# Feed-forward pairs: two of seven weight remainders on GpSimd, and a 4 KB scratch for dynamic DMAs

## Chip, cores and metric

One core of a Trainium2 chip runs the whole kernel. The metric is the device time of one execution in microseconds. The engines are named as in the profile: PE is TensorE (PEld its weight loads), DVE VectorE, ACT ScalarE, POOL GpSimd, SP the engine that issues most of the DMAs.

## What is computed

A two-layer encoder on 512 tokens of width 1024, in fp32. Each layer is a feed-forward, a mixer (attention of two kinds), attention to a memory, and a second feed-forward. The change touches the four feed-forwards alone:

```python
def swiglu(x, wg, wu, wd):
    return (jax.nn.silu(x @ wg) * (x @ wu)) @ wd

for layer in range(DEPTH):
    h = h + 0.5 * swiglu(rmsnorm(h, g), wg, wu, wd)      # ffn1
    h = h + mixer(rmsnorm(h, mix_g), ...)
    h = h + memory_xattn(rmsnorm(h, mg), rmsnorm(mem, sg), ...)
    h = h + 0.5 * swiglu(rmsnorm(h, g), wg, wu, wd)      # ffn2
```

wg and wu are 1024 x 2816, wd is 2816 x 1024.

## The kernel before

**Numbers in two parts.** A matrix product in fp32 is done as three products of numbers in a shorter form (fp32r in the code). Each operand t is split into h, its rounding to that form, and l = t - h, the remainder; the product is h·h + h·l + l·h. For a weight tile, ScalarE makes h (an activation that copies, L519 in the pairs, L167 elsewhere) and VectorE makes l (a tensor_sub, L520 and L169). In the mixers some of the L169 subtractions are given to GpSimd (`wshare`). In the feed-forwards `wshare` is 0, so there all are on VectorE.

**Pairs.** The 22 blocks of 128 hidden columns of wg and wu are taken two at a time. Pair 0 is plain (`plain_pair`). The other ten pairs of a feed-forward, p = 1 to 10, use a seven-product scheme (Strassen's) on 2 x 2 quarters: the weights of a pair come as four quarters of 128x1024, and the tokens as four quarters and four prepared sums. The products of a pair, in the order in which TensorE runs them, with the tokens' name in quotes:

- `open_pair`: "11" with quarter 0 (w11), into bank y
- `sum_pair`: "1" with quarter 2 + quarter 3 (s), into bank z; "2" with s - w11 (L580), into y
- `cross_pair`: "21" with **quarter 1** (w12), into a bank of its own; "3" with quarter 0 - quarter 2, into y
- then `open_pair` of the next pair
- `close_pair`: `lower`, "4" with **quarter 3**, into y; `upper`, "22" with w12 - s (L623), into z. In the last pair `upper` comes first.

Between the products into y and z the bank is copied into `gu` by ScalarE (L564, L587, L608, L619) or added to it by VectorE (L597, L609, L627). The pair ends with the gates (L656, Silu at L658, L659) and the split of the hidden values (L429 on ScalarE, L433 on VectorE).

A product (`product`, L541) is 24 matmuls of 128x128 weights on 256 columns: two halves of the output, in each four blocks with h·h, four with the tokens' l, four with the weights' l. So the weights' l is first read by the ninth matmul. The operand of a product lies in one of three places: two buffers of the tiles `wh`/`wl`, and one pair of own tiles `sh`/`sl` for every third.

**Sums made by DMA.** Quarter 2 + quarter 3 and quarter 0 - quarter 2 are made by a plain fetch on SP's queue (L528) followed by an accumulating DMA that GpSimd issues (L574, L603); for the second, ScalarE negates the fetched quarter first (L602). [...]

**First pair.** The prepared token sums are made at the start of a feed-forward (`token_sums`, L452) and split at first use (L459 on ScalarE, L462 and L464 on VectorE). R, the row of normalising factors, is copied from PSUM by VectorE (L406). In this pair the operand of "21" is queued by hand behind the remainder of "2":

```python
with self.tc.high_priority(), self.behind(f.lowered if p == 1 else None):
    pair.w12 = self.raw_quarter(p, 1)
    w = self.operand(pair.w12)
```

`behind(ins)` is `issue_after`: what the block issues on the engine of `ins` comes behind `ins` on that engine; it adds no wait, and nothing on other engines is held.

**Order of work.** TensorE's order is the order of the program. On the other engines a scheduler sets the order beforehand, from a simulated timeline, and takes work under `high_priority` first. On the chip every engine runs its queue in order, with waits on semaphores.

After pairs 4 and 8 and in the last, `down` multiplies the hidden values with wd (L685), with the results scaled by R and added to x (L695, L696).

Of the kernel before, what the change touches and what calls it, by code (L numbers as in the profile page):

```python
# [11 lines left out]
F32 = mybir.dt.float32  # L12
# [99 lines left out]
class Encoder:  # L112
# [392 lines left out]
        f.own = True  # L505
        return tiles

    def operand(self, t, own=None):

        nc, f = self.nc, self.f  # L510
        if own is None:
            own = f.n % 3 == 2
            f.n += 1
        if own:
            h, l = self.own_tiles()
        else:
            h, l = [self.wp.tile([P, 1024 + WHOLE], F32R, name=n, tag=n, bufs=2)[:, o:o + 1024]
                    for n, o in (("wh", LINE), ("wl", LINE + STEP))]
        self.leading = nc.scalar.activation(h, t, AF.Copy)  # L519
        self.parted = nc.vector.tensor_sub(l, t, h.bitcast(F32))  # L520
        return h, l

    def quarter(self, p, q):
# [65 lines left out]
    def cross_pair(self, pair):  # L589
        nc, f, p = self.nc, self.f, pair.p  # L590
        with self.tc.high_priority(), self.behind(f.lowered if p == 1 else None):
            pair.w12 = self.raw_quarter(p, 1)
            w = self.operand(pair.w12)
        x = self.bank("pa")
        self.product(x, w, self.tokens("21"), True)
        c = self.corner(pair, 0, 0)
        nc.vector.tensor_add(c, c, self.halves(x))  # L597
        with self.tc.high_priority():
            s = f.tp.tile([P, 1024], F32, name="s3", tag="s3", bufs=2)
            self.fetch(s, p, 2)  # L600
            with self.behind(f.led), self.behind(f.taken):
                nc.scalar.activation(s, s, AF.Copy, scale=-1.0)  # L602
            nc.gpsimd.dma_start(s, self.quarter(p, 0), accum_op=OP.add)  # L603
            w = self.operand(s)
            f.crossed = self.parted
        self.product(pair.y, w, self.tokens("3"), False)
        c = self.corner(pair, 1, 1)
        f.taken = nc.scalar.copy(c, self.halves(pair.y))  # L608
        nc.vector.tensor_add(c, c, self.halves(pair.z))  # L609

    def close_pair(self, pair, final):
        nc, f, p = self.nc, self.f, pair.p
        own = False if final else None

        def lower():
            with self.tc.high_priority():
                w = self.operand(self.raw_quarter(p, 3), own)
            self.product(pair.y, w, self.tokens("4"), False)
            nc.scalar.copy(self.corner(pair, 1, 0), self.halves(pair.y))  # L619

        def upper():
            with self.tc.high_priority(), self.behind(f.crossed if p == 1 else None):
                nc.vector.tensor_sub(pair.s, pair.w12, pair.s)  # L623
                w = self.operand(pair.s, own)
            self.product(pair.z, w, self.tokens("22"), False)
            c = self.corner(pair, 0, 1)
            nc.vector.tensor_add(c, c, self.halves(pair.z))  # L627

        gu = pair.gu.rearrange("p (b z t) -> p b z t", b=2, z=2)
        if final:  # L630
            gs2 = f.tp.tile([P, 1024], F32, name="gs", tag="gs")
            t2 = f.tp.tile([P, 1024], F32, name="t", tag="t")

            def gate(b):
                gs, t = (x[:, b * S:(b + 1) * S] for x in (gs2, t2))
                nc.vector.tensor_mul(gs, gu[:, b, 0, :], f.R)
                nc.scalar.activation(t, gs, AF.Silu)
                nc.vector.tensor_mul(gs, t, gu[:, b, 1, :])
                return gs

            upper()
            with self.tc.high_priority():
                gs = gate(0)
            lower()
            with self.tc.high_priority():
                self.hidden_parts(p, gs, 0)
                self.hidden_parts(p, gate(1), 1)
            return
        lower()
        upper()  # L650

        def gates(after=None):
            gs = f.tp.tile([P, 1024], F32, name="gs", tag="gs")
            two = lambda t: t.rearrange("p (b t) -> p b t", b=2)
            with self.behind(after):
                nc.vector.tensor_mul(two(gs), gu[:, :, 0, :], f.R.unsqueeze(1).to_broadcast([P, 2, S]))  # L656
            t = f.tp.tile([P, 1024], F32, name="t", tag="t")
            nc.scalar.activation(t, gs, AF.Silu)  # L658
            nc.vector.tensor_mul(two(gs), two(t), gu[:, :, 1, :])  # L659
            self.hidden_parts(p, gs, 0)  # L660

        return gates
# [1077 lines left out]
```

## Time and profile before

| | |
|---|---|
| time, median of 3 runs | 2048.16 us (2047.85 to 2049.57) |
| profiled execution, its own time | 2049.99 us |
| its span | 2048.2 us |
| granted TensorE clock | 0.999 |
| busy: PE, DVE, ACT, POOL | 2039.4, 1516.7, 1142.3, 356.5 us |
| share of the chain that ended last: PE | 96% |
| L520 on DVE, in all | 280 instructions of 1.22 us |
| L169 on POOL (mixers) | 43 instructions |
| accumulating DMAs that POOL issues | 80 |

Rows of the profile read as: start, duration, engine, line, operation, output <- inputs, shapes, count, and in brackets the idle time before it with what ended it. A group's row has minimum/median/maximum in ns. A row of waits has who waited, for whom, us in total, times, and the longest.

### The profile page before, as it was taken

The numbers are of one execution on the slowest core, as the hardware profiler recorded it, in microseconds if no ns is written. First come the engines' busy times: TensorE is split into PE (matmuls) and PEld (weight loads), VectorE is DVE, ScalarE is ACT, GpSimd is POOL, SyncE is SP. The second block draws the span as 40 slices with busy tenths as digits, with TensorE's granted clock in tenths as the row PEclk, the third lists the DMA queues.
The fourth block names the chain that finished last, engine by engine and source line by source line (L and its number), as shares of the span: only waits on it lengthen the run. The fifth ranks groups of instructions, "written<-read, shape, count | busy, mean of one in ns | idle before, by whom it ended". The sixth has DMA issues, their size and how long they took to land.

```text
span 2048.2 us, 32531 instructions
## 1 busy us (share of the span) xinstructions
PE 2039.4 (100%) x12845; PEld 1825.0 (89%) x12845; DVE 1516.7 (74%) x2199; ACT 1142.3 (56%) x1719; POOL 356.5 (17%) x323
## 2 busy tenths in 40 slices
PE   9999999999999999999999999999999999999999
PEld 7989898888888899998989899988888888989997
DVE  8858577799676797685789576685668688958676
ACT  7636354556785664462556264454768566626443
POOL 1101003355521110010020000013353111001000
PEclk9999999999999999999999999999999999999999
DMA  7847545322332176483456476444224324747543
GB/s 222 224 117 193 144 116 167 98 88 83 104 122 69 52 216 165 135 204 105 118 170 183 127 180 168 124 124 147 93 83 127 100 73 144 190 120 189 161 121 95
DMA packets 87272, 279.64 MB, mean 137 GB/s; under 512 B 9808, under 2 KB 13008, under 8 KB 87120
## 3 DMA queue, kind: packets, MB, share of 16 engines
q1 hardware_dynamic: 75312, 235.09, 35.5%
q0 software_dynamic: 11520, 41.95, 11.8%
q8 instruction: 101, 1.65, 0.3%
q14 instruction: 51, 0.42, 0.1%
q10 hardware_dynamic: 288, 0.52, 0.1%
HBM read 271.24 MB, written 6.29 MB: 135 GB/s over the span
## 4 chain that ended last, share of the span: by engine, by line
PE 96%; DVE 1%; DMA 1%; ACT 1%; issue 0%; POOL 0%; SPq 0%; DVEq 0%; POOLq 0%; ACTq 0%
PE ps_pa L541 26%; PE ps_pa L797 13%; PE ps_pa L685 12%; PE ps_pb L685 12%; PE ps_pb L541 11%; PE ps_pa L743 5%; PE ps_pb L910 3%; PE ps_pa L386 2%; PE ps_pa L1398 2%; PE ps_pa L1231 2%; PE ps_pb L963 1%; PE ps_pb L743 1%; PE ps_pb L936 1%; PE ps_pa L1130 1%; PE ps_pb L386 1%; DMA wf<-l_ffn_wq 1%
## 5 line engine op out<-in xcount | busy, mean ns | idle before, releaser
L167 ACT ACTIVATE wh<-wf 128x1024 fp32r<-128x1024 f32 (+2 forms) x219 | 216.2, 992 | 350.8 <-PE ps_pb L685 92.3
L169 DVE TENSOR_TENSOR wl<-wf,wh 128x1024 fp32r<-128x1024 f32 (+2 forms) x176 | 203.8, 1161 | 42.4 <-ACT wh L167 38.6
L519 ACT ACTIVATE wh<-s 128x1024 fp32r<-128x1024 f32 x108 | 114.9, 1064 | 110.3 <-PE ps_pa L541 41.0
L520 DVE TENSOR_TENSOR wl<-s,wh 128x1024 fp32r<-128x1024 f32 x108 | 132.1, 1223 | 58.7 <-ACT wh L519 57.1
L603 POOL DMA_DIRECT2D s<-l_ffn_wq x40 | 34.8, 870 | 761.6 <-ACT s L602 717.5
L519 ACT ACTIVATE wh<-wf 128x1024 fp32r<-128x1024 f32 x84 | 88.9, 1058 | 91.6 <-PE ps_pa L685 30.2
L797 PE MATMUL ps_pa<-wh,xh 128*128 128x512 f32 x384 | 121.7, 398 | 0.0
L797 PE MATMUL ps_pa<-wh,xl 128*128 128x512 f32 x384 | 118.9, 391 | 0.0
L797 PE MATMUL ps_pa<-wl,xh 128*128 128x512 f32 x384 | 118.7, 390 | 0.0
L169 POOL TENSOR_TENSOR wl<-wf,wh 128x1024 fp32r<-128x1024 f32 (+1 forms) x43 | 95.6, 2224 | 128.9 <-ACT wh L167 128.6
L695 DVE TENSOR_TENSOR dn<-ps_pa,R 128x512 f32<-128x512 f32 x48 | 33.1, 689 | 97.5 <-PE ps_pa L685 97.2
L520 DVE TENSOR_TENSOR wl<-wf,wh 128x1024 fp32r<-128x1024 f32 x84 | 102.5, 1221 | 3.1 <-ACT wh L519 3.1
L685 PE MATMUL ps_pb<-hh,wh 128*128 128x512 f32 x352 | 96.2, 389 | 0.0
L685 PE MATMUL ps_pb<-hl,wh 128*128 128x512 f32 x352 | 96.1, 389 | 0.0
L685 PE MATMUL ps_pb<-hh,wl 128*128 128x512 f32 x352 | 96.0, 389 | 0.0
L520 DVE TENSOR_TENSOR sl<-s,sh 128x1024 fp32r<-128x1024 f32 x52 | 64.4, 1239 | 33.3 <-ACT sh L519 33.1
L685 PE MATMUL ps_pa<-hh,wh 128*128 128x512 f32 x328 | 88.9, 390 | 0.0
L685 PE MATMUL ps_pa<-hl,wh 128*128 128x512 f32 x328 | 88.6, 389 | 0.0
L685 PE MATMUL ps_pa<-hh,wl 128*128 128x512 f32 x328 | 88.6, 389 | 0.0
L254 POOL TENSOR_TENSOR acc<-acc,sq 128x512 f32<-128x512 f32 (+1 forms) x31 | 46.6, 1504 | 237.0 <-ACT sq L253 236.4
L797 PEld LDWEIGHTS ps_pa<-wh,xl 128*128 128x128 f32 x384 | 72.1, 188 | 15.7
L797 PEld LDWEIGHTS ps_pa<-wl,xh 128*128 128x128 f32 x384 | 72.0, 188 | 15.6
(403 smaller groups left out, 5774.9 us busy)
## 6 DMA issues: line engine op xcount, KB each, us to landing
wf<-l_ffn_wq SPq DMA_DIRECT2D x120, 512.0 KB, 3.9
s<-l_ffn_wq SPq DMA_DIRECT2D x80, 512.0 KB, 4.6
s<-l_ffn_wq POOLq DMA_DIRECT2D x80, 512.0 KB, 7.4
wf<-l_ffn_wd SPq DMA_DIRECT2D x64, 512.0 KB, 4.4
wf<-l_w_in SPq DMA_DIRECT2D x48, 512.0 KB, 3.3
wf<-l_ffn_wd SPq DMA_DIRECT2D x32, 384.0 KB, 3.1
wf<-l_w_out SPq DMA_DIRECT2D x16, 512.0 KB, 3.3
bias<-bias SPq DMA_DIRECT2D x28, 256.0 KB, 2.7
```

What stands on the lines that cost most here:

```text
L167: self.leading = nc.scalar.activation(wh[:, sl], w[:, sl], AF.Copy)
L169: eng.tensor_sub(wl[:, sl], w[:, sl], wh.bitcast(F32)[:, sl])
L254: self.summed = (eng or nc.gpsimd).tensor_add(acc[:, :n], acc[:, :n], sq[:, :n])
L386: nc.tensor.matmul(p, w[a][:, k * P:(k + 1) * P], xs[k][c], start=k == order[0] and a == c == 0, stop=k == order[-1] and a == 1)
L519: self.leading = nc.scalar.activation(h, t, AF.Copy)
L520: self.parted = nc.vector.tensor_sub(l, t, h.bitcast(F32))
L541: self.nc.tensor.matmul(bank[:, sl], w[a][:, o:o + P], xs[k][b], start=first and z == a == b == k == 0, stop=z == a == 1 and k == KB // 2 - 1,
L685: self.nc.tensor.matmul(bank, w[a][:, j * P:(j + 1) * P], h, start=j == a == e == 0, stop=j == nb - 1 and (a, e) == ops[-1])
L743: nc.tensor.matmul(banks[dd], w[g, k // 2][a][:, o:o + P], parts(k)[b], start=k == first and a == b == 0, stop=k == last and a == 1)
L797: nc.tensor.matmul(banks[j], xs[k][a][:, j * P:(j + 1) * P], w[b][:, kk * 512:kk * 512 + 512], start=k == a == b == 0, stop=k == KB - 1 an ...
L910: nc.tensor.matmul(bank[:, o:o + n], a, b[:, :n], start=c == 0, stop=c == len(ops) - 1)
L1231: nc.tensor.matmul(banks[c][i], a[:, i * P:(i + 1) * P], b[:, c * 512:(c + 1) * 512], start=(k == 0 and n == 0), stop=(k == KB - 1 and n = ...
```

## The change

`operand` gets an argument that says which engine makes the remainder. `cross_pair` (quarter 1) and `lower` in `close_pair` (quarter 3) pass GpSimd; the other five operands of a pair stay as they were. The scratch of the dynamic DMAs is given as 4096 bytes of each partition instead of the default.

```diff
-    def operand(self, t, own=None):
+    def operand(self, t, own=None, eng=None):
...
         self.leading = nc.scalar.activation(h, t, AF.Copy)
-        self.parted = nc.vector.tensor_sub(l, t, h.bitcast(F32))
+        self.parted = (eng or nc.vector).tensor_sub(l, t, h.bitcast(F32))
         return h, l
...
         with self.tc.high_priority(), self.behind(f.lowered if p == 1 else None):
             pair.w12 = self.raw_quarter(p, 1)
-            w = self.operand(pair.w12)
+            w = self.operand(pair.w12, eng=nc.gpsimd)
...
             with self.tc.high_priority():
-                w = self.operand(self.raw_quarter(p, 3), own)
+                w = self.operand(self.raw_quarter(p, 3), own, nc.gpsimd)
...
-    nc = bacc.Bacc("TRN2", target_bir_lowering=False, num_devices=1)
+    nc = bacc.Bacc("TRN2", target_bir_lowering=False, num_devices=1, dynamic_dma_scratch_size=4096)
```

## Prediction

> **What bounds the kernel now.** I read the busy shares first, then the chain that ended last, then the waits of TensorE, then one stretch of the feed-forward pairs.
>
> ```profile
> PE 2039.4 (100%) x12845; PEld 1825.0 (89%) x12845; DVE 1516.7 (74%) x2199; ACT 1142.3 (56%) x1719; POOL 356.5 (17%) x323
> PE 96%; DVE 1%; DMA 1%; ACT 1%; issue 0%; POOL 0%; SPq 0%; DVEq 0%; POOLq 0%; ACTq 0%
> PE ps_pb L222 <- DVE identb L126: 1.6, 1, 1.6
> PE ps_pa L386 <- ACT xh L227: 1.6, 2, 0.8
> PE ps_pa L541 <- ACT gu L564: 0.5, 1, 0.5
> 1232.44 13.60 PE ps_pa L541 x120
> 1213.00:1232.00 19.00, 19.00 (x170) 19.00 (x169) 15.91 (x16) 12.23 (x14) 1.73 (x2) 1.00 0.76 192
> ```
>
> In order: two lines of the page, three of the waits, a piece of the chain in order of time, and a window with the busy us of PE, PEld, DVE, ACT and POOL. The reader is to see that the end is set by TensorE: it is 96% of the chain, and the three longest waits listed for it come to 3.7 us in 2048.2. L541 is the line of the pairs' products. 120 matmuls in 13.60 us are 113 ns each, so a product of 24 takes 2.72 us and a pair of seven products 19.04 us. In the last row, a stretch about one pair long, TensorE is busy all 19.00 us and VectorE only 15.91, at a granted clock of 1.00. VectorE holds nothing up there. So taking work off it has nearly nothing to win; what the change can do is make an operand late.
>
> The profiled execution took 2049.99 us (span 2048.2, 1.8 around it); the median of the runs is 2048.16. My sum is a difference, and I add it to the median.
>
> **What is moved, and its price.** There are 4 feed-forwards of 10 pairs. In each pair the remainder (l = t - h) of the operands of products "21" (second quarter, cross_pair) and "4" (fourth quarter, close_pair's lower) goes from VectorE to GpSimd: 80 instructions. No DMA is added, the conversion h stays on ScalarE.
>
> ```profile
> L520 DVE TENSOR_TENSOR wl<-wf,wh x84: 1216/1219/1227, 28.2 to 2006.0; 128x1024 fp32r<-128x1024 f32 x84
> L169 POOL TENSOR_TENSOR wl<-wf,wh x43: 1295/2399/2857, 342.7 to 1691.0; 128x1024 fp32r<-128x1024 f32 x35, 128x512 fp32r<-128x512 f32 x8
> 342.18 1.08 DVE L696 SCALAR_TENSOR_TENSOR x<-dn,x 128x512 f32<-128x512 f32 x1
> 342.68 2.86 POOL L169 TENSOR_TENSOR wl<-wf,wh 128x1024 fp32r<-128x1024 f32 x1
> 344.35 1.74 DVE L232 SCALAR_TENSOR_TENSOR xl<-x,cols,xh 128x512 fp32r<-128x512 f32 x1
> L232 DVE SCALAR_TENSOR_TENSOR xl<-x,cols,xh x64: 735/748/1781, 6.2 to 1714.8; 128x512 fp32r<-128x512 f32 x64
> ```
>
> The columns of the rows with a count are minimum/median/maximum in ns. The same subtraction at the same size costs 1.22 us on VectorE and 2.40 on GpSimd (L169, in the mixers). The three rows at 342 show more. GpSimd's subtraction starts during L696 on VectorE, which ends at 343.26, and ends at 345.54, 2.28 us after it. L232, dispatched at 344.35, then takes 1.74 us where 0.74 is usual, and ends at 346.09, 0.55 us after GpSimd. So when both engines read two SBUF tensors they take turns: GpSimd ends **2.28 us after the VectorE instruction that it found running**, and the next VectorE instruction of two SBUF inputs ends **0.19 us less than its own length after GpSimd**, for one of 1.22 us 1.03 after it. VectorE keeps no time: for each moved 1.22 us it stands up to about 2.1 us, unless it had nothing of that kind to do.
>
> **The steady pair.** One pair, on all engines:
>
> ```profile
> 1229.35 1.07 ACT L519 ACTIVATE wh<-wf 128x1024 fp32r<-128x1024 f32 x1 [0.75 <-PE ps_pb L541]
> 1229.63 0.86 POOL L574 DMA_DIRECT2D s<-l_ffn_wq  x1 [4.78 <-DMA s<-l_ffn_wq]
> 1230.38 1.22 DVE L623 TENSOR_TENSOR s<-wf,s 128x1024 f32<-128x1024 f32 x1
> 1232.65 1.22 DVE L656 TENSOR_TENSOR gs<-gu,R 128x1024 f32<-128x1024 f32 x1
> 1233.90 1.06 ACT L658 ACTIVATE t<-gs 128x1024 f32<-128x1024 f32 x1 [0.76 <-DVE gs L656]
> 1235.81 0.56 ACT L587 COPY gu<-ps_pa 128x512 f32<-128x512 f32 x1
> 1235.90 0.62 PE L541 MATMUL ps_pa<-xh,wl 128*128 128x256 f32 x4
> 1237.72 0.62 PE L541 MATMUL ps_pa<-t3h,wh 128*128 128x256 f32 x4
> 1241.34 1.23 DVE L520 TENSOR_TENSOR wl<-s,wh 128x1024 fp32r<-128x1024 f32 x1 [0.46 <-ACT wh L519]
> 1244.06 0.62 PE L541 MATMUL ps_pa<-t4h,wl 128*128 128x256 f32 x4
> 1244.00 1.22 DVE L520 TENSOR_TENSOR sl<-s,sh 128x1024 fp32r<-128x1024 f32 x1 [0.84 <-ACT sh L519]
> ```
>
> The h of "21" is ready at 1230.42, GpSimd has just issued its DMA (till 1230.49), VectorE is in L623 till 1231.60. GpSimd then ends at 1233.88; TensorE first reads this remainder at 1235.90, so 2.0 us are left. The gate product L656 ends at 1234.91 instead of 1233.87, 1.04 later. The Silu (L658), ScalarE's next conversion and the copy L587 all shift by that: the copy ends at 1237.41, and product "3", which writes on in the bank that it reads, starts at 1237.72. 0.3 us are left, the thinnest margin here. For "4", with h and the engines about 1 us late, GpSimd starts behind L433 at about 1240.1 and ends at 1242.4, needed at 1244.06. The remainder of "22" (1241.34) ends at about 1243.4 and the next one, at 1244.00, stands where it stood: the pair has caught up. **Cost 0** in the 36 pairs that follow a first one. The cover is operands prepared some 3 us ahead; without it each late one costs its lateness.
>
> **The first pair of each feed-forward** is another matter: there VectorE also makes the token sums' remainders (L462) and R (L406), without a pause, and the diff undoes an order. The block around "21" is queued behind the remainder of "2" when p is 1; such an order holds on one engine, so on GpSimd it holds nothing, and the subtraction starts as soon as its h is there. Feed-forward 1, then the rows that matter of 2, 3 and 4:
>
> ```profile
> 34.57 1.04 ACT L519 ACTIVATE wh<-wf 128x1024 fp32r<-128x1024 f32 x1
> 34.74 1.23 DVE L580 TENSOR_TENSOR s<-s,wf 128x1024 f32<-128x1024 f32 x1
> 35.88 1.22 DVE L462 TENSOR_TENSOR t2l<-tq,t2h 128x1024 fp32r<-128x1024 f32 x1
> 37.02 0.68 DVE L406 COPY R<-ps_pb 128x512 f32<-128x512 f32 x1
> 37.62 1.22 DVE L520 TENSOR_TENSOR sl<-s,sh 128x1024 fp32r<-128x1024 f32 x1
> 39.00 0.62 PE L541 MATMUL ps_pa<-t2h,sl 128*128 128x256 f32 x4
> 737.16 1.06 ACT L519 ACTIVATE wh<-wf 128x1024 fp32r<-128x1024 f32 x1 [1.33 <-DMA wf<-l_ffn_wq]
> 737.79 1.22 DVE L462 TENSOR_TENSOR t2l<-tq,t2h 128x1024 fp32r<-128x1024 f32 x1
> 741.69 0.63 PE L541 MATMUL ps_pa<-t2h,sl 128*128 128x256 f32 x4
> 1070.97 1.06 ACT L519 ACTIVATE wh<-wf 128x1024 fp32r<-128x1024 f32 x1 [3.04 <-PE ps_pa L541]
> 1071.10 1.22 DVE L462 TENSOR_TENSOR t2l<-tq,t2h 128x1024 fp32r<-128x1024 f32 x1
> 1075.33 0.62 PE L541 MATMUL ps_pa<-t2h,sl 128*128 128x256 f32 x4
> 1734.92 1.23 DVE L580 TENSOR_TENSOR s<-s,wf 128x1024 f32<-128x1024 f32 x1
> 1739.18 0.64 PE L541 MATMUL ps_pa<-t2h,sl 128*128 128x256 f32 x4
> ```
>
> Feed-forward 1: the remainder of "2" (sl, L520) ends at 38.84, 0.16 us before TensorE reads it at 39.00. With the change, "21" has its h at 35.61 and waits out L580 (till 35.97): GpSimd ends at 38.25. L462, the next to start, ends 1.03 later at 39.28, R about 0.6 later (its start overlaps by 0.08) at 39.88, sl at 41.02: TensorE waits 2.0 us. Feed-forward 4 has the same order: GpSimd ends at 1736.15 + 2.28 = 1738.43, sl 2.77 later at 1741.20, against 1739.18: 2.0 us. In 2 and 3 h comes during L462, which ends at 739.01 and 1072.32; R reads PSUM and passes, sl waits: 739.01 + 2.28 + 1.03 = 742.32 against 741.69, 0.6 us; 1072.32 + 3.31 = 1075.63 against 1075.33, 0.3 us. **Sum +4.9 us.** If GpSimd gets its turn only behind L462 in 1 and 4 too, sl ends at 37.10 + 3.31 = 40.41, and these two cost 1.4 each: sum 3.7. If "4" then meets the next pair's first remainder in the same way, VectorE's loss of about 0.9 comes once more in each: sum 8.5. I take 4.9, by the turn of the row at 342, and keep 0 (no turns) to 8.5.
>
> [...]
>
> Small terms, at nothing: GpSimd's own queue holds L574 and L603, the two accumulating transfers of a pair. L574 stands ahead of the moved subtraction (1229.63 above); should it come behind, it starts at 1233.9, 4.3 later, lands in 7.4 by the row below and still comes before that half's conversion, which ends at 1243.97. A weight tile is freed up to 1.2 us later; the fetch into it, issued at 1213.71, is the second quarter of the next pair, needed at 1229.35.
>
> ```profile
> 1213.71 0.33 SPq L528 DMA_DIRECT2D wf<-l_ffn_wq  x1
> s<-l_ffn_wq POOLq DMA_DIRECT2D x80, 512.0 KB, 7.4
> ```
>
> The smaller scratch has no row. [...] I take 0.
>
> **Rivals.** (A) The forecast: the first pairs stall, 2048.2 + 4.9 = 2053. (B) The stalls don't come, because GpSimd loses its turns to the uninterrupted VectorE or the queue is planned otherwise: 2048 (2047 to 2051). For it: nearly all of the 80 have slack; against: the row at 342 and the margin of 0.16. [...] (C) The 0.3 us of L587 goes as well: 0.3 to 0.5 us in each of 36 pairs, 11 to 18 more, about 2066. For it the thin margin; against, each pair catches up. (D) Faster: VectorE, freed in the first pairs, hands over R and the gates earlier. It decides only if GpSimd's reads pass beside VectorE's. Its price is capped by TensorE's waits, 3.7 us, of which 0.5 is in the pairs; beyond that, only another order of the mixers could bring it, to 2043.
>
> **How the numbers follow.** 0.2% is 4.1 us, about what a measurement of this kernel tells from no change. Chances: A 0.52 (of it 0.34 over 4.1 us), B 0.31, C 0.12, D 0.05. Slower 0.46, same 0.49, faster 0.05. The likeliest is A: 2053, its own range 2050 to 2057. From B's lower end towards C, leaving out D and C's upper half: 2046.5 to 2062.
>
> **What would show it.** Right: GpSimd subtractions of L520 at 2.4 us or more; VectorE instructions of 2 us or more beside them; in the first pairs sl of product "2" later than the matmul that needs it, and a wait of TensorE for it of 0.3 to 2 us; steady products still 2.72 us apart. Wrong: "2" on time, or products in later pairs over 2.72 us, or stretches outside the feed-forwards that moved.

## The result and the profile after

The changed kernel takes 2071.11 us (median; the kernel before 2048.05 beside it), a ratio of 1.012 (95% interval 1.0089 to 1.015): slower by 23 us or 1.2%, where 2053 was forecast within 2046.5 to 2062. The profiled execution took 2071.27 us with a span of 2069.2, 21.0 more than before.

Busy time of the engines after, and the groups of L520 on GpSimd and VectorE (busy us, mean ns of one):

```profile
PE 2044.0 (99%) x12845; PEld 1827.8 (88%) x12845; DVE 1539.2 (74%) x2119; ACT 1140.7 (55%) x1719; POOL 569.1 (28%) x403
L520 POOL TENSOR_TENSOR wl<-wf,wh 128x1024 fp32r<-128x1024 f32 x56 | 149.1, 2662 | 532.5 <-ACT wh L519 518.5
L520 DVE TENSOR_TENSOR wl<-s,wh 128x1024 fp32r<-128x1024 f32 x108 | 176.4, 1634 | 70.0 <-ACT wh L519 68.0
```

VectorE has 80 instructions fewer and is busy 22 us longer: the 108 remainders of this group take 1.63 us on the mean (1.22 before). The turns of the forecast are there, and VectorE gained nothing. But it still has idle time (it is busy 74% of the span), so the longer busy time is not by itself the loss; that is in the waits of TensorE:

```profile
PE ps_pa L541 <- POOL wl L520: 5.9, 4, 1.6
PE ps_pa L541 <- ACT gu L564: 5.4, 3, 1.8
PE ps_pa L541 <- DVE sl L520: 2.4, 4, 0.7
PE ps_pa L541 <- POOL sl L520: 1.9, 3, 0.8
...
PE ps_pa L541 <- ACT gu L587: 0.9, 1, 0.9
```

These five are new or grown, all at L541, the products of the pairs. A stall costs somewhat more than its wait, since matmuls beside it are slower: at 204.90 the wait is 1.60 us, and the second matmul behind it starts 227 ns after the first. So I took from the trace the starts of neighbouring matmuls of L541 and added up what lies over the usual 113 ns: 1.8 us in all before, 23.6 after. By place:

| what came late | where (us) | cost, us |
|---|---|---|
| remainder of "21", behind L574 in GpSimd's queue | 204.9, 913.5, 1252.3, 1920.8 (1.4 to 1.9 each); 791.7, 1129.9, 1231.4 and two small | 10.0 |
| product "2" of the first pair | 38.8, 747.1, 1087.0, 1756.6 (2.2, 3.9, 0.5, 2.3) | 8.9 |
| next "11" of the first pair | 49.0, 1096.2, 1766.8 (1.0 each) | 3.0 |
| copy L587 | 166.4, 773.7 (1.1, 0.1) | 1.3 |

The stretches between the pairs (mixers, products with wd) take the same time as before within 0.2 us each. In the other direction, one stretch at half clock near the start of the profiled execution before (8.15 to 11.56) is missing after, 1.3 us.

**The largest item.** GpSimd's queue around 205 us, before, then after:

```profile
187.75 0.86 POOL L603 DMA_DIRECT2D s<-l_ffn_wq  x1 [12.75 <-ACT s L602]
192.99 0.86 POOL L574 DMA_DIRECT2D s<-l_ffn_wq  x1 [4.38 <-DMA s<-l_ffn_wq]
```

```profile
187.99 2.54 POOL L520 TENSOR_TENSOR sl<-wf,sh 128x1024 fp32r<-128x1024 f32 x1 [4.35 <-ACT sh L519]
190.96 0.88 POOL L603 DMA_DIRECT2D s<-l_ffn_wq  x1 [0.43 <-ACT s L602]
201.59 0.86 POOL L574 DMA_DIRECT2D s<-l_ffn_wq  x1 [9.75 <-DMA s<-l_ffn_wq]
202.16 2.69 POOL L520 TENSOR_TENSOR wl<-wf,wh 128x1024 fp32r<-128x1024 f32 x1
```

The last row is the remainder of "21". Its h had been ready since 197.4, but the queue runs in order and L574, ahead of it, sits 9.75 us waiting for its fetch of s. The subtraction ends at 204.85 and TensorE goes on at 204.90, 1.9 us late. Before, L574 followed L603 by 5.24 us; now it follows by 10.63. SyncE's queue at the same place, before and after, shows the fetch that L574 waits for:

```profile
187.31 0.33 SPq L528 DMA_DIRECT2D s<-l_ffn_wq  x1
```

```profile
191.65 0.33 SPq L528 DMA_DIRECT2D s<-l_ffn_wq  x1
```

Before, the fetch of s went out 0.44 us ahead of L603's accumulating transfer (187.31 against 187.75) and landed in 5.1 us; after, it goes out 0.69 us behind it (191.65 against 190.96) and lands in 9.4. It waits for VectorE's remainder of "22", the last reader of the buffer; that one now takes its turn behind the remainder of "4" on GpSimd:

```profile
189.26 2.35 DVE L520 TENSOR_TENSOR wl<-s,wh 128x1024 fp32r<-128x1024 f32 x1 [0.44 <-ACT wh L519]
```

It ends at 191.61, 1.08 us behind GpSimd's end (190.53), and the fetch goes out at 191.65. L603 waits for ScalarE's L602 and has moved by 3.21 us, as all of this stretch has (its first product started at 193.5 before and at 196.7 after); the fetch has moved by 4.34. So 1.1 us of delay on VectorE's side swap two transfers.

**The first pairs.** VectorE, GpSimd and TensorE in feed-forward 1 after:

```profile
34.41 2.58 POOL L520 TENSOR_TENSOR wl<-wf,wh 128x1024 fp32r<-128x1024 f32 x1 [1.61 <-ACT wh L519]
34.60 3.46 DVE L462 TENSOR_TENSOR t2l<-tq,t2h 128x1024 fp32r<-128x1024 f32 x1
38.15 0.59 ACT L564 COPY gu<-ps_pa 128x512 f32<-128x512 f32 x1 [2.37 <-DVE t2l L462]
38.59 1.21 DVE L520 TENSOR_TENSOR sl<-s,sh 128x1024 fp32r<-128x1024 f32 x1
38.79 0.73 PE L541 MATMUL ps_pa<-t2h,sh 128*128 128x256 f32 x4 [1.79 <-ACT gu L564]
46.65 2.33 DVE L520 TENSOR_TENSOR sl<-wf,sh 128x1024 fp32r<-128x1024 f32 x1
49.04 0.73 PE L541 MATMUL ps_pa<-xh,sl 128*128 128x256 f32 x4 [0.73 <-DVE sl L520]
```

GpSimd ends at 36.99, L462 at 38.06, R and sl behind it: the forecast's chain to 0.1 us, shifted by the 1.3 us of the start. TensorE is stopped a step earlier than I wrote, though: the copy L564 waits for L462 too, and product "2" can't begin before it. Ten us later VectorE's remainder of the next "11" waits out "4" and is 1.0 us late.

**Half clock.** In feed-forward 2 the stall of product "2" cost 3.9 us. Windows of 3.41 us each, the length of the record at half clock (busy us of PE, PEld, DVE, ACT, POOL; granted clock), the second pair from another stall:

```profile
745.02:748.43 3.41, 1.59 (x12) 1.33 (x12) 3.41 (x4) 1.99 (x3) 0.23 (x1) 1.00 0.27 105
748.43:751.84 3.41, 3.41 (x18) 3.41 (x17) 3.41 (x5) 2.85 (x3) 0.00 (x0) 0.50 0.00 0
1250.18:1253.59 3.41, 1.79 (x16) 1.60 (x15) 3.41 (x2) 1.55 (x3) 2.06 (x1) 1.00 0.95 147
1253.59:1257.00 3.41, 3.41 (x33) 3.41 (x32) 3.41 (x4) 2.25 (x3) 0.41 (x1) 1.00 0.87 293
```

After a window in which TensorE was busy 1.59 us the granted clock is 0.50 for one window, with 18 matmuls in it instead of 33: 15 times 113 ns, 1.7 us. After 1.79 us nothing follows.

### The profile page after: what moved, and what is told of

It is laid out like the page before. It is cut to its first block, busy times and chain, and to the rows that moved or that the text cites. A ratio compares the mean times of both kernels' runs of the same rounds, so it can differ in the third digit from the quotient of the medians.

```text
span 2069.2 us, 32573 instructions
## 1 busy us (share of the span) xinstructions
PE 2044.0 (99%) x12845; PEld 1827.8 (88%) x12845; DVE 1539.2 (74%) x2119; ACT 1140.7 (55%) x1719; POOL 569.1 (28%) x403
## 3 DMA queue, kind: packets, MB, share of 16 engines
q8 instruction: 101, 1.65, 0.3%
## 5 line engine op out<-in xcount | busy, mean ns | idle before, releaser
L520 POOL TENSOR_TENSOR wl<-wf,wh 128x1024 fp32r<-128x1024 f32 x56 | 149.1, 2662 | 532.5 <-ACT wh L519 518.5
L520 DVE TENSOR_TENSOR wl<-s,wh 128x1024 fp32r<-128x1024 f32 x108 | 176.4, 1634 | 70.0 <-ACT wh L519 68.0
L574 POOL DMA_DIRECT2D s<-l_ffn_wq x40 | 36.2, 904 | 293.5 <-DMA s<-l_ffn_wq 140.6
L520 DVE TENSOR_TENSOR sl<-s,sh 128x1024 fp32r<-128x1024 f32 x52 | 70.1, 1349 | 47.7 <-ACT sh L519 45.7
L696 DVE SCALAR_TENSOR_TENSOR x<-dn,x 128x512 f32<-128x512 f32 x96 | 93.5, 974 | 0.9
```

Of the source, the lines that this page charges most:

```text
L520: self.parted = (eng or nc.vector).tensor_sub(l, t, h.bitcast(F32))
L574: nc.gpsimd.dma_start(pair.s, self.quarter(p, 2), accum_op=OP.add)
L696: x = nc.vector.scalar_tensor_tensor(self.x[d], t, 0.5, self.x[d], op0=OP.mult, op1=OP.add)
```

## Experiments

Theory after the profile: the turns of the two engines cost at two places, in the first pairs and where "21" stands behind L574. Rivals: the scratch; the length of the GpSimd subtraction by itself; rival (C), the copy L587.

**The scratch.** Before with the 4 KB scratch alone, and after with the scratch as it was:

```diff
+    nc = bacc.Bacc("TRN2", target_bir_lowering=False, num_devices=1, dynamic_dma_scratch_size=4096)   # before
-    nc = bacc.Bacc("TRN2", ..., dynamic_dma_scratch_size=4096)                                        # after
+    nc = bacc.Bacc("TRN2", ...)
```

> The kernel before with the 4 KB scratch alone, no subtraction moved. Theory (the moved subtractions cause the whole loss): within 0.2% of 2048, products still 2.72 us apart. Rival (the smaller scratch delays the accumulating DMAs, or moves tiles to worse addresses): L574 and L603 land later than the 7.4 us median of before, and a good part of the 23 us shows here.

> [...] Theory: about 2071, the same waits in the same places. Rival (scratch matters): clearly under 2071.

Measured: 2047.93 us, ratio 0.9997 (0.9987 to 1.0006), and 2073.88, 1.0124 (1.0109 to 1.0139). The scratch alone does nothing, and with the scratch of before the loss stays (2.8 us more than the changed kernel's median, within the spread of its runs, 2069.14 to 2080.32). The loss belongs to the moved subtractions.

**One of the two at a time.**

```diff
-                w = self.operand(self.raw_quarter(p, 3), own, nc.gpsimd)
+                w = self.operand(self.raw_quarter(p, 3), own)               # only "21" on GpSimd
-            w = self.operand(pair.w12, eng=nc.gpsimd)
+            w = self.operand(pair.w12)                                      # only "4" on GpSimd
```

> Only the remainder of product 21 on GpSimd, that of 4 back on VectorE, 4 KB scratch. Theory: two mechanisms meet. In the first pair GpSimd takes its turn ahead of L462 and of the remainder of 2, so product 2 waits about 2.1 us in feed-forwards 1, 2 and 4 and 0.5 in 3: +7. The other loss (21 stuck in GpSimd's queue behind L574, whose fetch is late because SP's queue stands at a weight tile that 4 on GpSimd frees late) needs both moves and goes away: L574 is again issued about 6 us before product 21. Sum about 2055 to 2057. Rival (each moved subtraction costs by itself through the turns with VectorE): half of the 23 us, 2059 to 2061, with stalls in the pairs before the second down.

> Only the remainder of product 4 on GpSimd, that of 21 back on VectorE, 4 KB scratch. Theory: SP's fetch into the tile that 4 frees, and the fetch of s behind it, are as late as in the changed kernel, so L574 is issued late (under 1 us before product 21 in the pairs before the second down), but nothing that TensorE needs stands behind it: no loss there. In the first pair the remainder of the next 11 waits its turn behind 4 for about 1 us in three feed-forwards: +3. Sum 2049 to 2052. Rival (each moved subtraction costs by itself): 2059 to 2061.

Measured: only "21" 2064.81 us, 1.0082 (1.0065 to 1.0098), more than expected; only "4" 2049.79, 1.0005 (0.9996 to 1.0015). In the first, "21" is late behind L574 just as well, only in other pairs (61.5, 81.3, 768.0, 787.8, 1104.8 and 1124.9 us): the theory that this needs both moves was wrong. In the second L574 is late too, but no work that TensorE needs soon stands behind it. By itself "4" costs nothing clear of the noise; "21" does.

**The two places.** First pair on VectorE again; L574 queued behind the remainder of "21" of the pair before; both; and the second with only "21" of the first pair on VectorE:

```diff
+            w = self.operand(pair.w12, eng=nc.gpsimd if p > 1 else None)        # first pair; "4" likewise
...
+            with self.behind(f.moved):                                          # f.moved: the remainder of "21" in cross_pair
+                nc.gpsimd.dma_start(pair.s, self.quarter(p, 2), accum_op=OP.add)  # L574
```

> The changed kernel, but with both remainders of pair 1 of each feed-forward on VectorE. Theory: the waits for product 2 (2.2, 3.9, 0.5, 2.3 us, with the stretch at half clock behind the second) and for the next 11 (about 1 us in three feed-forwards) go, some 11 us: 2059 to 2062. What stays are the waits of product 21 behind L574. Rival (the loss comes from all pairs alike): about 2069.

> The changed kernel, but with the accumulating DMA L574 of a pair queued on GpSimd behind the subtraction of 21 of the pair before. Theory: the subtraction of 21 starts when its h is there and has its 2.0 us of slack in every pair; the waits of 21 (10 us in the profile, with what follows them) go: 2059 to 2063; L574 is issued about when it was. Rival (the wait behind L574 hides a wait for VectorE's turn): still about 2070.

> Both: pair 1 on VectorE, and L574 queued behind 21 in the other pairs. Theory: 36 pairs still have two subtractions on GpSimd and cost nothing but a few waits at the copy L587 (about 1 us each in one or two pairs): 2048 to 2052. Rival (turns between the engines cost in each pair): 2055 or more.

> The changed kernel with the accumulating transfer of the next pair queued behind the remainder of 21 (as in the run at 2061.06) and the remainder of 21 of each first pair on VectorE; the remainder of 4 of the first pair stays on GpSimd. Theory that of the four first-pair stalls it is the remainder of 21 that makes product 2 late (2.27, 3.77, 0.54 and 2.24 us in that run) and the remainder of 4 that makes the next 11' late (1.03, 1.01, 1.02): the first kind goes, the second stays: 2051.7 + 3 = 2053 to 2056. Rival, that VectorE freed of one and blocked by the other only shifts the stall: 2058 to 2062.

| | us | ratio (95%) |
|---|---|---|
| first pair on VectorE | 2069.17 | 1.0104 (1.0087 to 1.012) |
| L574 behind "21" | 2061.06 | 1.0065 (1.005 to 1.008) |
| both | 2051.68 | 1.0017 (1.0008 to 1.0027) |
| L574 behind "21", only "21" of the first pair on VectorE | 2050.92 | 1.0016 (1.0006 to 1.0025) |

TensorE's waits at L541, with the first pair on VectorE:

```profile
PE ps_pa L541 <- POOL sl L520: 7.2, 6, 2.2
PE ps_pa L541 <- POOL wl L520: 4.6, 4, 1.5
PE ps_pa L541 <- ACT gu L587: 0.9, 1, 0.9
```

with L574 behind "21" (L588 is L587 there and in the next run):

```profile
PE ps_pa L541 <- ACT gu L564: 5.4, 3, 1.8
PE ps_pa L541 <- DVE sl L520: 2.5, 4, 0.7
PE ps_pa L541 <- ACT gu L588: 0.9, 1, 0.9
```

and with that and "21" of the first pair on VectorE:

```profile
PE ps_pa L541 <- DVE sl L520: 0.9, 1, 0.9
PE ps_pa L541 <- ACT gu L588: 0.9, 1, 0.9
```

The order of two entries in GpSimd's queue is worth 10.05 us (2071.11 to 2061.06), as the table of places has it, and the subtraction of "21" in the four first pairs 10.1 more. "4" of the first pair can stay on GpSimd: without "21" there, two of the three waits of the next "11" did not come either (the one of feed-forward 3 did, 1.2 us at 1083.6), so that run came out under its expectation of 2053 to 2056. The last two runs still lie 3.6 and 2.7 us above the kernel before; the copy L587 is 1.1 us of it in each, the rest was not followed. The first run was a miss: its first-pair stalls are gone, but the waits for GpSimd grew from 7.8 to 11.8 us. What was removed in one place came back at the other; the gains add up only once the queue is mended.

**Turns or queue?** The kernel before with the 4 KB scratch, VectorE keeping all its subtractions; at the same 80 places GpSimd also writes a tile that nobody reads, by the same subtraction, by a copy of one input, or by a fill:

```diff
+            nc.gpsimd.tensor_sub(spare, t, h.bitcast(F32))
+            nc.gpsimd.tensor_copy(spare, t)        # second run
+            nc.gpsimd.memset(spare, 1.0)           # third run
```

> The kernel before with the 4 KB scratch, all remainders on VectorE as before, and in addition the same two subtractions per pair on GpSimd into a spare tile that nobody reads (80 instructions whose result is not used). No operand waits for GpSimd. Theory of the turns: VectorE, 15.9 us busy of 19.0 in a pair, loses about 2.1 us at each of them and is over-full: TensorE waits in nearly every pair, 1 to 2 us each, 2080 to 2120. Rival (what hurts is only that GpSimd's results come late): 2048 to 2051.

> As the run with the 80 subtractions doubled, but GpSimd only copies the weight tile (one input in SBUF) into the tile that nobody reads; VectorE keeps every subtraction. Theory that the turns are taken against whatever GpSimd reads from SBUF: VectorE is held for the length of a copy, which is at most that of the subtraction (2.54 to 2.74 us): 2060 to 2115 us, and VectorE's subtraction of these lines still lengthens from 1.22 us. Rival, that the turn is taken only where GpSimd's operation has two inputs in SBUF: 2046 to 2052 us, as before, with VectorE's subtractions at 1.22 us.

> GpSimd only fills the unread tile with a constant at the same 80 places: it writes SBUF but reads nothing. If the turns are taken for GpSimd's reads: 2046 to 2053 us, as before, VectorE's subtractions at 1.22 us. If any GpSimd operation on SBUF takes its turn, or if what costs is the queue (an instruction ahead of an accumulating transfer on GpSimd): 2060 us or more, with waits for gu, sl and wl as in the run with the subtractions doubled.

Measured: 2123.38 us, 1.0367 (1.0352 to 1.0383); 2055.66, 1.004 (1.0025 to 1.0055); 2048.14, 0.9999 (0.9989 to 1.0008). In the first, nothing waits for GpSimd's result, yet:

```profile
PE ps_pa L544 <- ACT gu L590: 24.8, 17, 2.3
PE ps_pa L544 <- DVE sl L520: 12.0, 13, 1.8
PE ps_pa L544 <- DVE wl L520: 11.0, 15, 1.5
```

L590 is L587 of the other kernels, L544 the products. When VectorE keeps its work, the 80 subtractions in addition cost 75 us, a little over the range expected; VectorE is busy 1661.0 us (1516.7 before), and the longest of TensorE's waits is at the copy of rival (C). This run does not separate the turns from what 80 more entries do in GpSimd's queue. With the copy (groups), then with the fill (a piece in order of time, two engines):

```profile
L523 POOL COPY spare<-wf 128x1024 f32<-128x1024 f32 x80 | 122.7, 1533 | 528.9 <-DMA wf<-l_ffn_wq 528.6
L520 DVE TENSOR_TENSOR wl<-wf,wh 128x1024 fp32r<-128x1024 f32 x84 | 111.1, 1323 | 3.1 <-ACT wh L519 3.1
```

```profile
18.81 2.30 POOL L523 MEMSET spare<- 128x1024 f32 x2
18.68 1.23 DVE L169 TENSOR_TENSOR wl<-wf,wh 128x1024 fp32r<-128x1024 f32 x1 [0.46 <-PE ps_pa L386]
```

A copy still lengthens VectorE's subtractions (1.32 us on the mean against 1.22). The time of that run fell below what I had expected: the copy needs no h, starts as soon as the weights have landed, and its turns are short (1.53 us on the mean). Nor does that run show where its 7.5 us go: TensorE waits 0.5 us at the products, and 3.6 us at L405, at the start of a feed-forward, which I did not follow. The fills depend on nothing, so they ran ahead of the pairs, 13 in a row from 3.02 us, and say nothing about the queue. But 18 of VectorE's 128x1024 subtractions lay beside a fill, and none of them took over 1.23 us. So in these three runs VectorE's subtractions were held up by a GpSimd operation that reads SBUF, with one input too, and not by one that only writes: the 84 of the group shown took 1.65 us on the mean with the subtraction on GpSimd, 1.32 with the copy and 1.22 with the fill.

**Why the fetch of L574 is late.** Three tries to bring it forward: four buffers for the raw weights; three for s; and three with the fetch of s ahead of that of quarter 3 in the program:

```diff
-        ... name="wf", tag="wf", bufs=3)
+        ... name="wf", tag="wf", bufs=4)          # first
-            pair.s = f.tp.tile([P, 1024], F32, name="s1", tag="s1", bufs=2)
+            pair.s = f.tp.tile([P, 1024], F32, name="s1", tag="s1", bufs=3)   # second, third
+                    f.early = self.early_sum(p + 1)      # third: tile and fetch of the next pair's s
+                w = self.operand(self.raw_quarter(p, 3, None if final else self.loaded), own, nc.gpsimd)
```

> The changed kernel with four buffers instead of three for the raw weight quarters. Theory that the remainder of 21 is late because GpSimd ends 4 late, so that the weight tile comes free late, so that SyncE waits for it with the fetch of s behind it in its queue, so that the accumulating transfer ahead of 21 starts late: SyncE no longer waits, the fetch of s lands in about 5.1 us again, the accumulating transfers start some 5 us earlier, and TensorE's waits for the remainder of 21 (7.8 us in the changed kernel, with 3 to 4 us of slowed stretch beside them) go: 2058 to 2064 us, like the run that reordered GpSimd's queue (2061.06). Rival, that the fetch is late for another reason (DMA engines shared with the transfers that GpSimd issues): the landings stay at 7 to 9 us, and the time at 2068 to 2074.

> The changed kernel with three buffers instead of two for the tile s whose accumulating transfer (L574) stands ahead of the remainder of 21; SyncE's order is left. Theory 1, that the fetch of s is late because its buffer is freed by VectorE's subtraction of product 22, which in turn waits out GpSimd's remainder of 4: the fetch goes out before L603's transfer, lands in about 5 us, L574 runs some 4 us earlier and the waits for the remainder of 21 (7.8 us and slowed stretches) go: 2058 to 2064 us. Theory 2, that it is late because it stands in SyncE's queue behind the fetch of the weight tile that GpSimd's remainder of 4 frees: the fetch of s comes at most 1 us earlier and the time stays within 2064 to 2071.

> As the run before with three buffers of s, and the fetch of the next pair's s put ahead of the fetch of product 4's weight quarter in SyncE's queue. By theory 1 and by theory 2 alike the fetch now goes out some 4 to 6 us earlier, ahead of L603's transfer, and the remainder of 21 is no longer late: 2058 to 2064 us, TensorE's waits for GpSimd's wl and sl under 1 us. Rival, that the accumulating transfers are slow by themselves beside each other, whenever the fetch goes out: 2066 to 2073.

Measured: 2068.54 us, 1.0098 (1.008 to 1.0116); 2074.23, 1.0124 (1.0106 to 1.0142); 2075.14, 1.0125 (1.0109 to 1.0141). All three missed what the theory expected, and only the first came out as its rival said: the fetch stayed where it was. With three buffers of s one more L574 runs at the start of the feed-forward (18.3, 21.0 and 27.7 us, where the changed kernel has 18.2, 20.7 and then 55.1), and from there SyncE fetches for one pair later, at the same place, behind the same release. SyncE's waits there with three buffers:

```profile
SPq L528 <- POOL sl L520: 4.9, 1, 4.9
SPq L528 <- DVE wl L520: 0.7, 1, 0.7
```

The scheduler had spent the buffer on running further ahead. The last two also lie 3 to 4 us above the changed kernel's median, outside every expectation, though within the spread of its runs; both have new waits of TensorE at the start of a feed-forward (L405, 3.0 and 3.1 us), which I did not follow. So I left the buffers, and changed only which transfer goes first, by two fills of an unread tile between the remainder of "4" and L603:

```diff
+                with self.behind(f.four):                  # f.four: the remainder of "4" of the pair before
+                    nc.gpsimd.memset(spare, 1.0)
+                with self.behind(f.four):
+                    held = nc.gpsimd.memset(spare, 1.0)
+            with self.behind(held):
                 nc.gpsimd.dma_start(s, self.quarter(p, 0), accum_op=OP.add)   # L603
```

> The changed kernel with two fills of an unread tile (0.99 us each on GpSimd, nothing read) put into GpSimd's queue between the remainder of 4 and L603, from the second pair of each feed-forward on, so that L603's accumulating transfer goes out some 2 us later and the fetch of s is issued first again, as before the change; nothing else is moved. Theory, that L574 is late because its fetch is issued 0.7 us behind L603 instead of 0.4 us ahead of it and shares the DMA engines with it: the fetch lands in 5 to 6 us instead of 9, L574 starts 3 to 4 us earlier, TensorE's waits for the remainder of 21 (7.8 us) fall to under 2: 2058 to 2064 us. Rival, that the order of the two transfers does not matter: the fetch still lands in 8 to 9 us and the time is 2068 to 2076 (the fills cost GpSimd 2 us a pair more).

Measured: 2062.01 us, 1.0064 (1.0047 to 1.008): 9 us less than the changed kernel, for 2 us of useless work a pair. GpSimd's queue at the place shown above:

```profile
188.02 2.53 POOL L520 TENSOR_TENSOR sl<-wf,sh 128x1024 fp32r<-128x1024 f32 x1 [5.58 <-ACT sh L519]
190.50 0.96 POOL L607 MEMSET spare<- 128x1024 f32 x1
191.51 0.96 POOL L609 MEMSET spare<- 128x1024 f32 x1
192.41 0.88 POOL L611 DMA_DIRECT2D s<-l_ffn_wq  x1
197.69 0.86 POOL L574 DMA_DIRECT2D s<-l_ffn_wq  x1 [4.40 <-PE ps_pb L299]
198.26 2.72 POOL L520 TENSOR_TENSOR wl<-wf,wh 128x1024 fp32r<-128x1024 f32 x1
```

SyncE's fetch of s goes out at 191.67, 0.02 from where it was, but now ahead of L603 (here L611). It lands in 5.5 us, L574 starts at 197.69 instead of 201.59, and the remainder of "21" 3.9 us earlier. No wait of TensorE for GpSimd is left in this run. (Its row of L574 names a matmul behind the wait; the fetch landed at 197.1.) At this place, then, the order of the two transfers makes L574 late. Over the whole trace of the changed kernel, the ten fetches of s that went out 0.44 to 1.34 us ahead of L603 landed in 4.2 to 6.6 us, the eleven that went out 0.47 to 0.88 us behind it in 6.5 to 9.4; of the eleven in between some landed in 3.7 us and some in 8.9, so the order is not all.

In the run with only "21" on GpSimd, L574 is late without "4" there. Its trace shows the two transfers close together as well: at the six places the fetch went out between 0.15 us ahead of L603 and 0.26 us behind it and landed in 7.6 to 9.0 us. Ahead of the second of them VectorE's subtraction at 59.06 took 3.52 us beside "21", and the fetch came 1.36 us later than before (68.97), L603 only 0.80 (68.78). So it seems that "21" alone can swap the two; no run tested that.

No run came out faster than the kernel before; TensorE was busy for nearly all of its span there, and little was to be won.

## Why the prediction was wrong

**Right.** TensorE sets the end, and VectorE's freed time is worth nothing. The turns are those of the rows at 342: in the changed kernel GpSimd's subtraction ended 2.30 to 2.38 us behind the VectorE instruction of this size that it found running (49 times; 2.28 forecast), and VectorE's next one 1.08 to 1.09 behind GpSimd (57 times; 1.03 forecast). The steady pair, where L574 is on time (feed-forward 2 of the changed kernel):

```profile
868.17 3.39 POOL L520 TENSOR_TENSOR wl<-wf,wh 128x1024 fp32r<-128x1024 f32 x1 [0.33 <-ACT wh L519]
873.58 0.62 PE L541 MATMUL ps_pa<-xh,wl 128*128 128x256 f32 x4
874.60 0.56 ACT L587 COPY gu<-ps_pa 128x512 f32<-128x512 f32 x1
875.39 0.62 PE L541 MATMUL ps_pa<-t3h,sh 128*128 128x256 f32 x4
```

The remainder of "21" has 2.0 us left, as forecast, and the copy 0.23 (0.3 forecast). R passes beside GpSimd, as forecast: in feed-forward 3 L406 (1083.46) took its usual 0.68 us during a subtraction of GpSimd's (1083.34 to 1085.85). Rival (C)'s copy is late at two places only, for 1.3 us. The scratch, at 0 in the forecast as an estimate, does nothing (2047.93 us with it alone).

**The step that failed** is the cost of 0 for the 36 pairs behind a first one, and in it "Small terms, at nothing", on GpSimd's own queue. I saw that L574 stands ahead of the moved subtraction, and checked what the subtraction does to L574, not what L574 does to it. I also took its start (1229.63, 0.8 us before h is ready) as given. That start hung on a fetch that had been issued 0.44 us ahead of another transfer; VectorE's turn of 1.1 us, which I had worked out for "22" and called caught up, moved it behind. With that the cost of 0 in the 36 pairs became 10.0 us, which the run with L574 behind "21" gave back (10.05); the forecast's own sign of being wrong, products in later pairs over 2.72 us apart, is what came.

**Terms mis-sized.** Product "2" of the first pairs: forecast 2.0, 0.6, 0.3 and 2.0, measured 2.2, 3.9, 0.5 and 2.3. The two of 2.0 held. In feed-forward 2, GpSimd got its turn ahead of L462, which took 3.47 us there as in 1 and 4 (its start, 742.59, lies before 742.86), so 0.6 became 2.2, and a window at half clock added 1.7. I had no term for the clock. "4" against the next pair's first remainder, which I had at 0.9 in each as an upper end only, came in three of four, 1.0 each, where "21" was on GpSimd too, and in one of four without it. Together 4.9 became 11.9 (8.9 and 3.0).

Rival (A)'s place was right and its size was not. Rival (C)'s 2066 lies nearest to the 2071 measured, but that is luck: its copy cost 1.3 us, not 11 to 18. The range had no term for a compute instruction that shares a queue with waiting transfers.

## What to carry to other kernels

Before an instruction is put into a queue that also holds waiting DMA triggers, find what each trigger waits for and by how much its source leads the next transfer: a lead of 0.4 us is a margin like any other. A GpSimd operation that reads SBUF held up VectorE's next subtraction until about its own end here (it ended 1.08 us behind, and takes 1.22 alone), and the subtractions whose result nobody needs cost more than the moved ones (75 us against 23). An extra buffer does not move a transfer forward if the scheduler uses it to run one step further ahead, as with three buffers of s; look at the releaser in the trace, which stays the same.

## What the runs showed of the hardware

Two transfers at once, at the place shown: the plain fetch of 512 KB landed in 5.1 us issued 0.44 us ahead of the accumulating one, in 9.4 issued 0.69 us behind it; with L603 held back so that the fetch led by 0.75 us, in 5.5.

Where the clock fell to half in the pairs, it did so for one window of 3.41 us, behind one in which TensorE was busy 1.30 to 1.67 us. Of the run with the early fetch of s, then of the run with L574 behind "21":

```profile
741.22:744.63 3.41, 1.30 (x13) 1.10 (x11) 1.42 (x3) 0.42 (x1) 1.96 (x2) 1.00 1.04 274
744.63:748.04 3.41, 3.41 (x18) 3.41 (x17) 2.35 (x3) 2.59 (x3) 1.40 (x1) 0.50 1.06 249
```

```profile
743.45:746.86 3.41, 1.67 (x13) 1.41 (x12) 3.41 (x4) 1.98 (x3) 1.08 (x2) 1.00 0.59 120
746.86:750.27 3.41, 3.41 (x18) 3.41 (x17) 3.41 (x5) 2.84 (x3) 0.00 (x0) 0.50 0.49 96
```

Busy 1.30, 1.59 and 1.67 us were followed by half clock, as was 1.40 later in the run with the early fetch (1253.22 to 1256.63); 1.79 was not, and in the run with four weight buffers 1.65 us (35.05 to 38.46) was not either. At the start of the kernel, among other matmuls, 1.96 us (4.74 to 8.15, the kernel before) was followed by half clock, 2.16 us (4.32 to 7.73, after) was not. No single bound divides these numbers. In two executions the half-clock windows begin a whole number of windows apart: 512.00 us in the run with the early fetch, 150 times 3.413, and 2037.8 in the kernel before (8.15 and 2045.90), 597 times. In the changed kernel the matmuls on the two sides of product "2"'s stall start 2.06 us apart in feed-forward 1 and 2.10 in 2, and the stalls cost 2.2 and 3.9 us. Counted in windows from the one at half clock, the first lies across two, with TensorE busy 1.97 and 3.08 us (35.04 to 41.87), and no half clock follows; the second lies in the one of 1.59 us. That such a stall costs 2 us or 3.9 by where it falls in the windows is my estimate from these numbers.
